# The first pair of products split a third time, with its operands fetched by DMA instead of by matmul

## The chip, the cores and the metric

The kernel runs on one core of one Trainium2 chip. The metric is the device time of one execution in microseconds (us). A core has five engines that run beside each other: TensorE (PE in the profile; its weight loads are PEld), VectorE (DVE), ScalarE (ACT), GpSimd (POOL) and SyncE (SP). DMAs are issued from the queues of SyncE, ScalarE and GpSimd. Matmuls write to PSUM banks; all other operands are in SBUF or in DRAM.

## The reference

```python
def reference(x, router_logits, expert_weights):
    probs = softmax(router_logits, axis=-1)          # [16, 512, 8]
    for e in range(8):
        expert_out = np.matmul(x, expert_weights[e]) # [16, 512, 512] @ [512, 2048]
        output += probs[:, :, e:e+1] * expert_out
    return output                                    # [16, 512, 2048], f32
```

With the 8192 tokens as rows this is one product of a matrix Z (8192 x 4096) by a matrix W (4096 x 2048). Z holds x times the routing weight of each of the eight experts side by side, W the experts' weights on top of each other. The inputs are f32; the kernel multiplies in f16 and accumulates in f32.

## The kernel before, in words

**Three levels of splitting.** The product is not computed block by block. Rows (256 tokens each, even and odd), the sum over experts (0 to 3, 4 to 7) and columns (two halves of 1024) are halved, and seven products of sums of blocks take the place of eight. They are called 1 to 7, and each runs for 16 pairs of row blocks (q from 0 to 15). `STEPS = (1, 5, 6, 2, 7, 3, 4)` is the same splitting a second time: inside a product there are seven steps of 8 matmuls, each with 128 x 128 of Z as the weight load and 512 columns of W. `by_thirds` is the third level: for a stage of two products, steps 1 and 5 of both (32 matmuls of 512 columns) are replaced by 14 small products of 4 matmuls with 256 columns. Their left operands are sums of the two products' z halves (`Thirds`, made on VectorE as tasks 5, 6, 3, 7), their right operands are sums of quarters of the weight block (`third_sums`).

**Stages.** `stages` lists the pairs of products in order of time, and `run(stage)` emits one. Stage 0 is product 1 of q = 2 and 3, stage 1 product 1 of q = 4 and 5, and so on up to stage 6. Before this change `thirds` holds stages 1 to 6 of these seven (line 1584), so stage 0 runs its 14 steps whole. Product 1 of q = 0 and 1 comes ahead of all stages and is computed directly: lines 266 to 358 make four blocks `z0` by matmul with diagonal matrices of routing weights (`early_z0`), and two loops over the column halves n with four experts e each run 16 matmuls per expert. The kernel starts there, since these need only a quarter of x's first rows, a tiny softmax and the first casts of weights.

**Operands of stage 0.** A z half is x transposed (`xT`) times the routing weights broadcast over partitions (`pT`); `times` makes one on VectorE. For stage 0, `early_xp1` (lines 286 to 294) makes both with TensorE: four 128-column matmuls against an identity for xT, one 512-column matmul of ones against diagonal tiles for pT, copied out of PSUM by VectorE and ScalarE. The routing weights for it come from a small softmax of its own (`early_p(1)`, on `lg0[1]`). For all later stages xT is made by DMA transposes on SyncE and pT is loaded, broadcast over the partitions, from `p_dram`. `softmax_of_all` (lines 309 to 322) fills `p_dram`: it runs the softmax of all logits on VectorE and ScalarE, casts it to f16 on ScalarE (lines 319 and 320), and stores it from SyncE in four DMAs.

**Weights.** `cast_block` and `cast_w` issue DMAs on GpSimd's queue that read f32 weights and write f16. The four blocks `b11` of product 1 and the eight early x blocks (`cast_x`) are issued in one row at the very start, lines 230 to 242. `behind` holds a DMA back until what was issued before it.

**What sets the order.** VectorE's and ScalarE's instructions keep program order throughout (`dve`, `act`); the other engines' do so from line 360 on. VectorE's work in the stages is a `queue` of tasks with assumed costs. `clock` holds the assumed time of TensorE and of VectorE; `slack` moves TensorE's clock on and emits tasks while VectorE's is behind, and `need` emits all tasks up to the one that TensorE is about to read. Lines 1599 to 1607 fill this queue for stage 0: z halves, the weight sums 6, 7 and 4 of product 1 (`inner_sums`), the differences `s2`.

Of the kernel before, what the change touches and what calls it, by code (L numbers as in the profile page):

```python
# [31 lines left out]
def kernel(  # L32
# [7 lines left out]
    nc = tc.nc  # L40
    P = 128
# [64 lines left out]
    def dve(i):  # L106
        last[i.ins.engine] = i.ins
        tc.keep_in_program_order(i)
# [3 lines left out]
    def tt(o, a, b, op):  # L112
        dve(nc.vector.tensor_tensor(out=o, in0=a, in1=b, op=op))  # L113
# [9 lines left out]
    def sp(o, i):  # L123
        note(nc.sync.dma_start(out=o, in_=i))
# [10 lines left out]
    def mm(ps, z, w, start, stop):  # L135
        note(nc.tensor.matmul(ps, z, w, start=start, stop=stop, skip_group_check=True))  # L136
# [80 lines left out]
    def cast_x(j):  # L217
        pool(xs0[:, ds(j, 2), :], x_f[ds(j * HQ, HQ), :].rearrange(ROWS[j // 4], p=P))

    def load_lg0(t):  # L220
        rows = lg_f.rearrange("(q h) e -> q h e", h=2 * HQ)[ds(2 * t, 2), 0:HQ]
        tile_ = lg0[t].rearrange("p (q j) e -> p q j e", j=2)
        if t == 0:
            sp(tile_, rows.rearrange("q (p j) e -> p q j e", p=P))
        else:
            for q in range(2):
                sp(tile_[:, q], rows[q].rearrange("(j p) e -> p j e", p=P))
    lg0 = [cpool.tile([P, 4, E], f32, name=f"lg0_{t}") for t in range(2)]
    load_lg0(0)
    cast_x(0)  # L230
    cast_x(2)
    ident = cpool.tile([P, P], f16, name="ident")
# [2 lines left out]
                            pattern=[[-1, P]], channel_multiplier=1)  # L235
    b11 = {kn: new_w() for kn in BLOCKS}
    with behind():
        for kn in BLOCKS[:3]:
            cast_block(11, kn, b11[kn], 2 if kn == (0, 0) else 1)
    cast_x(4)  # L240
    cast_x(6)
    cast_block(11, BLOCKS[3], b11[BLOCKS[3]])

    def early_p(t):
        if t == 0:
            return softmax(lg0[t], 4, cpool.tile([P, HE, 4], f16, name="ph0"))
        pf = softmax(lg0[t], 4, cpool.tile([P, HE, 4], f32, name="pf0"))
        odd = pf.rearrange("p e (q j) -> p e q j", j=2)[:, :, :, 1]
        tt(odd[:, 0:2], odd[:, 0:2], odd[:, 2:4], ADD)
        ph = cpool.tile([P, HE, 4], f16, name="ph1")  # L250
        dve(nc.vector.tensor_copy(ph, pf))
        return ph

    def diag(p):

        d = h_tile([P, 4, P], f16)
        tt(d, ident.unsqueeze(1).to_broadcast([P, 4, P]), p.to_broadcast([P, 4, P]), MUL)
        return d
# [5 lines left out]
            dve(nc.vector.tensor_copy(o, ps))  # L264

    z0 = [zpool.tile([P, HE, C, P], f16, name="z", tag="z") for j in range(4)]
    ph0 = [early_p(0)]

    def diag_e(e):
        return diag(ph0[0][:, e].unsqueeze(2))  # L270

    def early_z0(e, d):
        for j in range(4):
# [5 lines left out]
    ones = cpool.tile([P, P], f16, name="ones")  # L279
    nc.vector.memset(ones, 1.0)  # L280
    xp1 = [[xpool.tile([P, C, HQ], f16, name=name, tag="x") for name in ("xT", "pT")] for t in range(2)]

    def diag_j(j):
        return diag(ph0[1][:, :, ds(j % 4, 1)])

    def early_xp1(j, d):
        t, rows = j // 2 - 2, ds(j % 2 * P, P)
        ps = (bank, bank2)[j % 2]()
        for c in range(C):
            mm(ps[:, ds(c * P, P)], xs0[:, j, ds(c * P, P)], ident, c == 0, c == C - 1)  # L290
        evacuate(xp1[t][0][:, :, rows], ps.rearrange("p (c t) -> p c t", c=C), 0)
        ps = (bank, bank2)[j % 2]()
        mm(ps, ones, d.rearrange("p e t -> p (e t)"), True, True)
        evacuate(xp1[t][1][:, :, rows], ps.rearrange("p (e t) -> p e t", e=HE), 1)

    R = 4
    J = HQ // R
# [3 lines left out]

    def load_logits():
        dve(nc.vector.memset(lg_all[:, 0, 0:1], 0.0))
        dve(nc.vector.memset(lg0[1][:, 0, 0:1], 0.0))
        load_lg0(1)
        for r in range(R):
            sp(lg_all[ds(r * NHQ, NHQ)], lg_v[r])

    def softmax_of_all():

        pf = softmax(lg_all, J, h_tile([P, E, J], f32))
        pq = h_tile([P, HE, J], f32)
# [7 lines left out]
        act(nc.scalar.copy(ph[:, E:], pq))  # L320
        for r in range(R):
            sp(p_dram[:, :, ds(r * J, J)], ph[ds(r * NHQ, NHQ)])

    kept = [dram.tile([2, HQ, NB], f32, name=f"kept_{i}") for i in range(NI)]

# [5 lines left out]
    for n in range(2):  # L331
        ps = [bank2() if n == 0 and j < 2 else bank() for j in range(4)]
        for e in range(HE):
            if n == 0 and e < 2:
                early_z0(e + 2, ds_[e + 2])
                if e == 0:
                    ds_.append(diag_e(3))
            if n == 0 and e == 2:
                ph0.append(early_p(1))
                ds_ = [diag_j(j) for j in range(4, 8)]  # L340
                softmax_of_all()
                w, sums = inner_sums(b11, new_w())
                third = {1: third_sums(w[1])}
            for c in range(C):
                for j in range(4):
                    mm(ps[j], z0[j][:, e, c], b11[e // 2, n][:, e % 2 * C + c, :],
                       e + c == 0, e == HE - 1 and c == C - 1)
            if n == 1:
                for j in ((4, 5), (6, 7), (), ())[e]:
                    early_xp1(j, ds_[j - 4])  # L350
                if e == 0:
                    sums[5]()
                elif e == 1:
                    third[5] = third_sums(w[5])
        for j in range(4):
            o = half()
            act(nc.scalar.copy(o, ps[j]))
            sp(kept[j // 2][n].rearrange("(p j) m -> j p m", j=2)[j % 2], o)

    ordered[0] = True  # L360
    SLOT = 1.73
# [1 line left out]
    HP = HQ // 2  # L363
    LAG, LATE, LATE_TWOS = 0.3, 2.6, 1.6
    queue = deque()
    clock = {"pe": 0.0, "dve": 0.0}

    class Task:

# [429 lines left out]


    right = {r: Right() for r in (2, 5, 6, 7, 4, 3)}
    right[1] = Right(w, {p: Task(2.29, sums[p]) for p in (6, 7, 4)})
    lefts, xs, ps_, bases = {}, {}, {}, {}

    def xblock(h):
# [775 lines left out]
            post(p)  # L1581
    finish.step, finish.post = step_at_end, post_at_end

    for stage in range(1, ND):
        thirds[stage] = Thirds(*(p.left for p in stages[stage]), third)
    for stage in range(ND + 1, last2):
        thirds[stage] = Thirds(*(p.left for p in stages[stage]), third2)
# [9 lines left out]
    for stage in range(k3 + 1, end):  # L1597
        thirds[stage] = Thirds(*(p.left for p in stages[stage]), third3, room_w, False)
    need_first = [right[1].task[p] for p in (6, 7, 4)]
    for p in (2, 3):  # L1600
        lefts[1, p].queue_make(0)
    queue.append(need_first[0])
    for p in (2, 3):
        lefts[1, p].queue_s2()
    for p in (2, 3):
        lefts[1, p].queue_make(1)
    queue.extend(need_first[1:])
    start_loads(1)
    store_loads(0)
# [31 lines left out]
```

## Time and profile before

| what | us |
|---|---|
| median of three runs (lowest, highest) | 1351.76 (1351.49, 2032.81) |
| the profiled execution | 1351.78 |
| its span, first to last instruction | 1350.1 |
| TensorE busy | 1344.0 |
| VectorE busy | 1166.9 |
| ScalarE busy | 281.9 |
| GpSimd busy | 403.9 |

The span is what the profile shows; the profiled execution's own time is 1.7 us longer. One of the three runs took 2032.81 us and stands apart from the other two, which agree within 0.3 us. The lines of the profile use the program's names: `out<-in`, with the tile's name and without its number. `z` is an operand of Z, `w` a block of weights, `ps` and `pt` are PSUM banks, `d` the differences s2, `h` a scratch tile. Nearly every VectorE line stands under L113 and every matmul under L136, since two helpers record them; one tells them apart by tiles and shapes. The granted TensorE clock was 1.0 throughout.

### The profile page before, as it was taken

The page shows a single profiled execution, that of the slowest core. Times are in us where ns is not written, and L with a number is a line of the kernel's source. Part 1 is how long each engine was busy: PE and PEld are TensorE (multiplying, and loading weights), DVE is VectorE, ACT ScalarE, POOL GpSimd, SP SyncE. Part 2 cuts the span into 40 slices and gives each one's busy share as a digit, 9 for nine tenths or more (in the row PEclk, how much of TensorE's full clock was granted, in tenths as well). Part 3 has the DMA queues.
Part 4 walks back from the last instruction along what each step waited for, and adds up shares of the span by engine and source line. Part 5 has one row for each costly group of instructions (what it writes and reads, how often), then busy time and mean ns, then how long its engine had stood idle before and what let it go on. Part 6 is the DMA issues. An engine that isn't in the chain of part 4 may idle for free.

```text
span 1350.1 us, 19508 instructions
## 1 busy us (share of the span) xinstructions
PE 1344.0 (100%) x7122; PEld 694.3 (51%) x7122; DVE 1166.9 (86%) x1483; ACT 281.9 (21%) x593; POOL 403.9 (30%) x619
## 2 busy tenths in 40 slices
PE   9999999999999999999999999999999999999998
PEld 4465655565544444444444444554555455556564
DVE  7878898989989889797897889889898989898984
ACT  3342423223211111111111100110111111224331
POOL 3123322333323232323312112424334231232342
PEclk9999999999999999999999999999999999999999
DMA  9999989989899999999998889999999989999997
GB/s 181 242 222 240 239 264 242 291 284 290 247 329 282 323 288 286 295 306 265 318 325 265 295 313 189 243 239 216 244 249 226 219 219 310 308 178 230 262 163 132
DMA packets 185392, 346.26 MB, mean 256 GB/s; under 512 B 52176, under 2 KB 81616, under 8 KB 181200
## 3 DMA queue, kind: packets, MB, share of 16 engines
q0 software_dynamic: 84960, 176.72, 58.0%
q1 hardware_dynamic: 97024, 146.15, 35.4%
q10 hardware_dynamic: 3312, 22.15, 4.6%
q8 instruction: 55, 0.90, 0.3%
q14 instruction: 41, 0.34, 0.1%
HBM read 203.19 MB, written 174.26 MB: 280 GB/s over the span
## 4 chain that ended last, share of the span: by engine, by line
PE 98%; DMA 1%; POOL 0%; issue 0%; ACT 0%; POOLq 0%
PE ps L136 77%; PE pt L136 21%; DMA w<-in_expert_weights_dram 1%; POOL w L127 0%; ACT h L1578 0%; POOL ident L234 0%; POOLq L234 0%; POOLq L1625 0%
## 5 line engine op out<-in xcount | busy, mean ns | idle before, releaser
L136 PE MATMUL ps<-w,z 128*128 128x512 f16 (+1 forms) x3884 | 840.0, 372 | 0.0
L136 PEld LDWEIGHTS <-z 128*128 128x128 f16 x5236 | 512.3, 98 | 538.1 <-issue 1.1
L127 POOL DMA_DIRECT2D out_dram<-h x380 | 251.8, 679 | 723.9 <-ACT h L751 321.9
L113 DVE TENSOR_TENSOR h<-ps,h 128x512 f32<-128x512 f32 x318 | 214.9, 686 | 59.1 <-PE ps L136 58.0
L136 PE MATMUL pt<-w,z 128*128 128x512 f16 (+1 forms) x1304 | 253.2, 338 | 0.7 <-DMA w<-in_expert_weights_dram 0.7
L113 DVE TENSOR_TENSOR z<-xT,pT 128x2048 f16<-128x2048 f16 x188 | 226.8, 1217 | 2.2 <-DMA xT<-xs 2.2
L136 PE MATMUL ps<-w,d 128*128 128x512 f16 x880 | 200.7, 379 | 0.0
L738 ACT COPY h<-ps 128x512 f32<-128x512 f32 x102 | 59.8, 586 | 394.0 <-PE ps L136 394.0
L136 PEld LDWEIGHTS <-d 128*128 128x128 f16 x880 | 86.1, 98 | 96.3
L113 DVE TENSOR_TENSOR z<-z,d 128x2048 f16<-128x2048 f16 x110 | 131.8, 1217 | 0.0
L113 DVE TENSOR_TENSOR w<-w 128x1024 f16<-128x1024 f16 (+2 forms) x106 | 116.1, 1114 | 2.6 <-PE ps L136 1.0
L113 DVE TENSOR_TENSOR d<-z 128x1024 f16<-128x1024 f16 x110 | 74.1, 685 | 1.0
L113 DVE TENSOR_TENSOR h<-pt,h 128x512 f32<-128x512 f32 x75 | 51.3, 687 | 27.0 <-PE pt L136 23.9
L751 ACT COPY h<-ps 128x512 f32<-128x512 f32 x54 | 31.6, 586 | 203.5 <-PE ps L136 203.5
L113 DVE TENSOR_TENSOR ps<-ps,h 128x256 f32<-128x256 f32 (+1 forms) x84 | 50.6, 603 | 21.0 <-PE ps L136 15.1
L734 ACT COPY h<-ps 128x512 f32<-128x512 f32 x89 | 49.9, 599 | 70.1 <-PE ps L136 61.3
L127 POOL DMA_DIRECT2D kept<-h x56 | 30.6, 547 | 86.2 <-DVE h L113 48.7
L113 DVE TENSOR_TENSOR z<-z 128x2048 f16<-128x2048 f16 (+1 forms) x52 | 50.5, 978 | 1.5
L730 ACT COPY ps<-ps 128x512 f32<-128x512 f32 x47 | 26.8, 570 | 107.4 <-PE ps L136 59.5
L113 DVE TENSOR_TENSOR h<-h 128x512 f32<-128x512 f32 (+2 forms) x69 | 45.0, 675 | 0.1
L127 POOL DMA_DIRECT2D out_dram<-kept x40 | 42.0, 1150 | 0.2 <-issue 0.2
L136 PEld LDWEIGHTS <-h 128*128 128x128 f16 x384 | 37.6, 98 | 4.3
(109 smaller groups left out, 691.7 us busy)
## 6 DMA issues: line engine op xcount, KB each, us to landing
out_dram<-h POOLq DMA_DIRECT2D x380, 256.0 KB, 7.5
z<-z SPq DMA_DIRECT2D x56, 512.0 KB, 8.7
pT<-p_dram SPq DMA_DIRECT2D x93, 256.0 KB, 8.1
h<-kept SPq DMA_DIRECT2D x88, 256.0 KB, 7.2
w<-wd ACTq DMA_DIRECT2D x20, 1024.0 KB, 8.6
w<-in_expert_weights_dram POOLq DMA_DIRECT2D x33, 512.0 KB, 12.2
xT<-x SPq DMA_DIRECT2D x63, 256.0 KB, 7.8
h<-out_dram SPq DMA_DIRECT2D x60, 256.0 KB, 8.9
```

Source lines behind the costliest of these rows:

```text
L113: dve(nc.vector.tensor_tensor(out=o, in0=a, in1=b, op=op))
L127: note(nc.gpsimd.dma_start(out=o, in_=i, **how))
L136: note(nc.tensor.matmul(ps, z, w, start=start, stop=stop, skip_group_check=True))
L730: act(nc.scalar.copy(self.banks["b"], x))
L734: act(nc.scalar.copy(o[tn], q if p == 5 else x))
L738: act(nc.scalar.copy(o[TN[p]], b if p == 2 else x))
L751: act(nc.scalar.copy(o[tn], b))
```

## The change

Stage 0 joins the stages that are split a third time, and its operands come another way:

- The small softmax, the diagonal tiles, the 16 transposing and 4 broadcasting matmuls of `early_xp1` and their copies are gone, and so are the two loads of `lg0[1]`.
- `softmax_of_all` is emitted earlier, at the second expert of the first column half. Its four stores to `p_dram` are issued by ScalarE, behind the two casts.
- `second_x` issues four transposing DMAs on SyncE that make xT of stage 0 from the early x blocks 4 to 7. `second_p` issues two loads of pT of stage 0 from `p_dram` on ScalarE, behind the evacuations of the first column half.
- The casts of x blocks 4 to 7 go ahead of the second half of the third weight block.
- Weight sums 5 and 6 of product 1 are made in halves; the queue for stage 0 is now the first half of sum 6, then `thirds[0].queue()` (z halves 0, sums 5, 6, 3, 7, s2, z halves 1) with the second half of sum 6 put in behind the sums, then weight sums 7 and 4. VectorE's assumed clock starts at -7.5.

```diff
-    load_lg0(0)
+    lg0 = cpool.tile([P, 4, E], f32, name="lg0")
...
-        for kn in BLOCKS[:3]:
+        for kn in BLOCKS[:2]:
             cast_block(11, kn, b11[kn], 2 if kn == (0, 0) else 1)
+        cast_w(11, BLOCKS[2], 0, b11[BLOCKS[2]][:, ds(0, C), :])
     cast_x(4)
     cast_x(6)
+    cast_w(11, BLOCKS[2], 1, b11[BLOCKS[2]][:, ds(C, C), :])
     cast_block(11, BLOCKS[3], b11[BLOCKS[3]])
...
-        dve(nc.vector.memset(lg0[1][:, 0, 0:1], 0.0))
-        load_lg0(1)
...
         for r in range(R):
-            sp(p_dram[:, :, ds(r * J, J)], ph[ds(r * NHQ, NHQ)])
+            act(nc.scalar.dma_start(out=p_dram[:, :, ds(r * J, J)], in_=ph[ds(r * NHQ, NHQ)]))
+
+    def second_p():
+        for t, (_, p) in enumerate(xp1):
+            act(nc.scalar.dma_start(out=p, in_=p_dram[2 * t + 4, ds(P1, HE), :].partition_broadcast(P)))
+
+    def second_x():
+        for j in range(4):
+            note(nc.sync.dma_start_transpose(out=xp1[j // 2][0][:, :, ds(j % 2 * P, P)], in_=xs0[:, j + 4, :]))
...
                 if e == 0:
                     ds_.append(diag_e(3))
+                else:
+                    softmax_of_all()
+                    second_x()
             if n == 0 and e == 2:
-                ph0.append(early_p(1))
-                ds_ = [diag_j(j) for j in range(4, 8)]
-                softmax_of_all()
...
             if n == 1:
-                for j in ((4, 5), (6, 7), (), ())[e]:
-                    early_xp1(j, ds_[j - 4])
                 if e == 0:
-                    sums[5]()
+                    sums[5](ds(0, C))
+                    sums[5](ds(C, C))
...
+        if n == 0:
+            second_p()
...
-    clock = {"pe": 0.0, "dve": 0.0}
+    clock = {"pe": 0.0, "dve": -7.5}
...
-    right[1] = Right(w, {p: Task(2.29, sums[p]) for p in (6, 7, 4)})
+    right[1] = Right(w, {p: Task(2.29, sums[p]) for p in (7, 4)})
+    right[1].task[6] = Task(1.22, lambda: sums[6](ds(C, C)))
...
-    for stage in range(1, ND):
+    for stage in range(ND):
         thirds[stage] = Thirds(*(p.left for p in stages[stage]), third)
...
-    for p in (2, 3):
-        lefts[1, p].queue_make(0)
-    queue.append(need_first[0])
...
+    later(1.22, lambda: sums[6](ds(0, C)))
+    thirds[0].queue()
+    queue.insert(7, need_first[0])
     queue.extend(need_first[1:])
```

More of the change, by code (lines that the diff above doesn't have):

```diff
@@ L218, in cast_x @@
         pool(xs0[:, ds(j, 2), :], x_f[ds(j * HQ, HQ), :].rearrange(ROWS[j // 4], p=P))
[L220 to L228, printed above, removed]
-    load_lg0(0)
+    lg0 = cpool.tile([P, 4, E], f32, name="lg0")
+    sp(lg0.rearrange("p (q j) e -> p q j e", j=2),
+       lg_f.rearrange("(q h) e -> q h e", h=2 * HQ)[ds(0, 2), 0:HQ].rearrange("q (p j) e -> p q j e", p=P))
     cast_x(0)
@@ L237 @@
     with behind():
-        for kn in BLOCKS[:3]:
+        for kn in BLOCKS[:2]:
             cast_block(11, kn, b11[kn], 2 if kn == (0, 0) else 1)
+        cast_w(11, BLOCKS[2], 0, b11[BLOCKS[2]][:, ds(0, C), :])
     cast_x(4)
     cast_x(6)
+    cast_w(11, BLOCKS[2], 1, b11[BLOCKS[2]][:, ds(C, C), :])
     cast_block(11, BLOCKS[3], b11[BLOCKS[3]])
[L244 to L252, printed above, removed]
     def diag(p):
@@ L266 @@
     z0 = [zpool.tile([P, HE, C, P], f16, name="z", tag="z") for j in range(4)]
-    ph0 = [early_p(0)]
+    ph0 = softmax(lg0, 4, cpool.tile([P, HE, 4], f16, name="ph0"))
     def diag_e(e):
-        return diag(ph0[0][:, e].unsqueeze(2))
+        return diag(ph0[:, e].unsqueeze(2))
     def early_z0(e, d):
@@ L277, in early_z0 @@
             evacuate(z0[j][:, e], ps.rearrange("p (c t) -> p c t", c=C), j)
-    ones = cpool.tile([P, P], f16, name="ones")
-    nc.vector.memset(ones, 1.0)
     xp1 = [[xpool.tile([P, C, HQ], f16, name=name, tag="x") for name in ("xT", "pT")] for t in range(2)]
[L283 to L294, printed above, removed]
     R = 4
@@ L1599 @@
     need_first = [right[1].task[p] for p in (6, 7, 4)]
-    for p in (2, 3):
-        lefts[1, p].queue_make(0)
-    queue.append(need_first[0])
[L1603 to L1606, printed above, removed]
+    later(1.22, lambda: sums[6](ds(0, C)))
+    thirds[0].queue()
+    queue.insert(7, need_first[0])
     queue.extend(need_first[1:])
```

## The prediction

> **What bounds the kernel now.** First the page: which engine never rests, and what the chain that ended last is made of.
>
> ```profile
> span 1350.1 us, 19508 instructions
> PE 1344.0 (100%) x7122; PEld 694.3 (51%) x7122; DVE 1166.9 (86%) x1483; ACT 281.9 (21%) x593; POOL 403.9 (30%) x619
> PE 98%; DMA 1%; POOL 0%; issue 0%; ACT 0%; POOLq 0%
> ```
>
> TensorE is busy throughout and the chain is TensorE for 98%. So TensorE time taken out is won in full, and a TensorE wait put in is lost in full; other engines count only where TensorE waits for them. All that the change touches lies in the first 65 us, so I went on to the timeline of TensorE there, then to the busy time of stretches cut where TensorE changes its work (columns: stretch, length, then busy time of PE, PEld, DVE, ACT, POOL).
>
> ```profile
> 17.33 0.59 PE L136 MATMUL ps<-w,z 128*128 128x512 f16 x2
> 18.26 0.59 PE L136 MATMUL pt<-w,z 128*128 128x512 f16 x2 [0.33 <-DMA w<-in_expert_weights_dram]
> ...
> 33.83 10.52 PE L136 MATMUL ps<-w,z 128*128 128x512 f16 x48
> 44.19 3.62 PE L136 MATMUL pt<-w,z 128*128 128x512 f16 x16
> 47.64 3.62 PE L136 MATMUL ps<-w,d 128*128 128x512 f16 x16
> 51.09 7.07 PE L136 MATMUL ps<-w,z 128*128 128x512 f16 x32
> ```
> ```profile
> 28.62:29.49 0.87, 0.87 (x11) 0.64 (x10) 0.45 (x1) 0.23 (x1) 0.00 (x0) 1.00 1.25 207
> 32.95:33.83 0.88, 0.88 (x12) 0.64 (x11) 0.46 (x1) 0.24 (x1) 0.00 (x0) 1.00 1.38 214
> ```
>
> From 44.19 to 47.64 there are 16 matmuls, 0.216 us each. The row of 48 holds the last 32 matmuls of the direct blocks and 16 of stage 0, so stage 0 starts at 33.83 + 32 x 0.216 = 40.74. Its step 2 starts at 51.09, and step 7 of its first product 16 matmuls later, at 54.54. I measure the change against that 54.54.
>
> **What TensorE is spared.** The two short stretches are the transposes and broadcasts by matmul that the change drops: 0.87 + 0.88 = 1.75 us. Steps 1 and 5 of both products are 32 matmuls, 6.91 us. What replaces them is seen in stage 1, which is already split a third time:
>
> ```profile
> 64.91 1.04 PE L136 MATMUL pt<-w,z 128*128 128x256 f16 x8
> ...
> 71.02 3.62 PE L136 MATMUL ps<-w,d 128*128 128x512 f16 x16
> ```
>
> That is 6.11 us, so 0.80 is spared. The wait at 18.26 is for a weight cast:
>
> ```profile
> 5.13 13.09 DMA w<-in_expert_weights_dram
> ```
>
> The dropped second small logits tile took 512 rows of 32 B (8 experts in f32) out of the same DMA engines just ahead of it. The gain is between 0 and 0.5 us (the pair at 17.33 is two matmuls of 0.216, so the next could have started at 17.76); I take 0.3. Sum: 2.85 us. If nothing new waited, stage 0 would start at 40.74 - 1.75 - 0.3 = 38.7, and the profiled time would be 1348.9.
>
> **What is late next: the routing weights.** They now make a round trip. Before, pT of stage 0 came out of a matmul; now it needs softmax of all logits, two casts, four stores to DRAM and a load.
>
> ```profile
> 13.84 1.29 DVE L264 CAST z<-ps 128x512 f16<-128x512 f32 x2 [2.35 <-PE ps L136]
> ...
> 19.28 0.68 DVE L200 TENSOR_REDUCE h<-h 128x64 f32<-128x512 f32 x1
> ```
> ```profile
> 25.25 0.40 ACT L320 CAST h<-h 128x256 f16<-128x256 f32 x1
> ```
> ```profile
> 9.44 1.43 SPq L124 DMA_DIRECT2D h<-in_router_logits_dram  x3
> 25.68 2.67 SPq L124 DMA_DIRECT2D p_dram<-h  x4
> 28.46 14.22 SPq L124 DMA_DIRECT2D kept<-h  x8
> 42.73 1.24 SPq L124 DMA_DIRECT2D pT<-p_dram  x2
> 45.03 6.28 SPq L432 DMA_TRANSPOSE xT<-xs  x4
> ```
>
> VectorE keeps program order, and the softmax now follows the last early z casts, which end at 13.84 + 1.29 = 15.13. The small softmax and four diagonal tiles between 15.1 and 19.28 are gone. Its input is there in time: the last of the four large logits loads, issued at 10.42, landed 5.9 us later at 16.3 (row below), with the 32 B rows ahead of it; without them I take it as in by 15.1 (1.2 later if not). From the first reduction to the first store were 25.68 - 19.28 = 6.4 us. So the stores are issued, now by ScalarE, from 21.5 to 24.2.
>
> The landing is the weak point. The answers on DMA, for 10.4 to 10.9 (loads of logits), 27.7 to 28 (the last store), 25.6 to 29.7, and 29.8 to 33:
>
> ```profile
> h<-in_router_logits_dram SPq DMA_DIRECT2D x1, 64.0 KB, 5.9
> p_dram<-h SPq DMA_DIRECT2D x1, 48.0 KB, 8.9
> q1 hardware_dynamic: 1, 0.00, 0.0%
> ...
> q0 software_dynamic: 621, 0.61, 112.1%
> q1 hardware_dynamic: 610, 0.08, 30.2%
> ```
>
> Until 29.7 not one packet of the stores had moved (4.1 us after the first issue); then they went one for one with the weight casts, 610 in 3.2 us, 190 per us. Four stores of 48 KB in 128 B pieces are 1536 packets: 8.1 us. In the changed kernel the casts run the whole time: 21.5 + 4.1 + 8.1 + 0.5 to land = 34.2. The transposes are then a third flow, so up to 35.5. By the last store's own 8.9 us it would be 23.5 + 8.9 = 32.4. I take 34.5. ScalarE waits for it before issuing the loads; behind them on ScalarE are the four evacuations after the second column half, needed at 38.7, so that wait itself costs nothing. The loads, at 42.7 and at 51.4, and over the whole run:
>
> ```profile
> pT<-p_dram SPq DMA_DIRECT2D x2, 256.0 KB, 5.3
> pT<-p_dram SPq DMA_DIRECT2D x2, 256.0 KB, 4.2
> DMA to landing us min/median/max: 3.3/8.1/20.0
> ```
>
> With 4.7, the first pT lands at **L = 39.2**, the second 0.6 later. Bounds: 32.4 + 3.3 = 35.7, and 35.5 + 5.9 = 41.4.
>
> The Trainium skill, "DMA: Bandwidth & Descriptors", section "Latency and other measured facts", speaks for a fast trip: about 0.6 us to the first byte of a hardware-queued transfer and some 2 us of fixed cost. By an estimate from that page the whole trip would be in by about 30 and the first rival below would come true; the 4.1 us without a packet says otherwise, under this load.
>
> The other additions. First the x casts that the transposes read, as GpSimd issues them, and the answers on their landing:
>
> ```profile
> 8.06 0.79 POOL L127 DMA_DIRECT2D w<-in_x_dram  x1
> 10.21 0.72 POOL L127 DMA_DIRECT2D w<-in_x_dram  x1 [1.36 <-DMA w<-in_expert_weights_dram]
> ```
> ```profile
> w<-in_x_dram POOLq DMA_DIRECT2D x1, 256.0 KB, 18.7
> w<-in_x_dram POOLq DMA_DIRECT2D x1, 256.0 KB, 17.9
> ```
>
> They landed at 26.8 and 28.1, 1.3 us apart for 256 KB, so a 512 KB cast takes 2.6. **Transposes:** the x casts now stand one 512 KB cast earlier in that row, and land at about 24.2 and 25.5. Four transposes at 1.57 us of issue (6.28 for 4) are out by 31, and with up to 7 us to land (an estimate: a third more than the 5.3 of pT) are all in by 38, ahead of L; two us more would still be hidden behind the first half's 1.2 us. The kept stores, next on SyncE, go out 2 us later; nobody waits for them. **Weights:** the second half of the third block lands in the place of the second x cast, at about 28, and is needed at 28.62 - 0.3 = 28.3, because no matmul of the dropped kind stands before it any more; sharing with the transposes may cost it 1 us, and that wait only takes from the one below. **Fourteen small products** bring ScalarE eight short copies more for the four casts of pT that go, hidden since TensorE waits for VectorE there, and VectorE the work below.
>
> **What TensorE then waits for.** With pT at L, VectorE has to do in this order: two z halves, the sums 5, 6, 3, 7, half of weight sum 6, two s2, four small evacuations, two z halves, weight sums 7 and 4, then the operand of step 7. From the VectorE timeline:
>
> ```profile
> 42.78 2.36 DVE L113 TENSOR_TENSOR z<-xT,pT 128x2048 f16<-128x2048 f16 x2
> 45.05 4.49 DVE L113 TENSOR_TENSOR w<-w 128x4096 f16<-128x4096 f16 x2
> 49.45 2.36 DVE L113 TENSOR_TENSOR z<-z,d 128x2048 f16<-128x2048 f16 x2
> ...
> 68.67 0.87 DVE L113 TENSOR_TENSOR ps<-pt,z 128x256 f32<-128x256 f32 x2 [2.52 <-PE pt L136]
> ...
> 74.65 0.69 DVE L113 TENSOR_TENSOR h<-z 128x1024 f16<-128x1024 f16 x1
> ...
> 77.31 1.29 DVE L113 TENSOR_TENSOR d<-z 128x1024 f16<-128x1024 f16 x2
> ```
>
> Two z halves 2.3; four sums 77.31 - 74.65 = 2.66; half a weight sum 1.1; two s2 1.2; four evacuations 1.6; two z 2.3; two weight sums 4.4; the operand 1.2. Sum 16.8, with semaphores 17.0. TensorE's own way to that step is a start at L + 1.2, 8 us for the split with its waits for the sums, and four steps of 1.73: L + 16.1, so VectorE decides: step 7 starts at **L + 17.0**. Before, VectorE was done with these sums at 51.8, 2.7 us ahead of step 7, because the matmuls of 28.6 and 33 gave it pT. So the change costs (L + 17.0) - 54.54 = L - 37.5. With L = 39.2 that is **+1.7 us**: the 2.85 spared are lost in about 4.5 us of waits in stage 0. Later VectorE has slack again: sums of stage 1 end at about L + 26, before that stage starts at L + 27.5. The profiled execution took 1351.78 (span 1350.1 and 1.7 around it), the median is 1351.76; so 1351.8 + 1.7 = **1353.5**.
>
> **Rivals.**
> *The trip is short* and TensorE keeps what it is spared. Even from L = 37.5, all 2.85 us won from L = 34.6 on: 1349 to 1351.8, at L = 35.7 1350.0. For it: the last store took 8.9 us, not 11; ScalarE's queue is empty, while SyncE's had loads ahead. Against: the 4.1 us with no packet. Chance 0.25.
> *The DMA engines are shared by three.* Casts, transposes and stores each get a third until the casts end at about 36, and the transposes and 1 MB of kept stores go on beside the loads: L of 41 to 43, so +3.5 to +5.5, 1355.3 to 1357.3. It decides from L = 41. The Trainium skill, same page, section "Issuing engines are not separate DMA queues", has that queues of several engines end on the same 16 DMA engines, so that moving the stores to ScalarE's queue brings no bandwidth; the one-for-one packet rows agree. Chance 0.2.
> *It does not do what it says*: large logits in only at 16.3, or the transposes later than pT, so that the earlier softmax is not earlier. Worth at most 1.2 us, 1354.7; inside the forecast's range.
>
> **How the numbers follow.** Forecast (L from 37.5 to 41, 1351.8 to 1355.3): 0.52. Short trip 0.25; three flows 0.2; 0.03 for something else. With both signs likely the range reaches into both: **1349.6 to 1356.4**; the likeliest case alone is 1351.8 to 1355.3. Two per cent is 27 us, about what a measurement of this kernel can tell from no change, and several times any wait here: faster 0.01, same 0.98, slower 0.01.
>
> **What would show it.** Gone: the 128-wide matmuls at 28.6 and 33. Stage 0 with 56 matmuls of 256 columns. VectorE idle for some 6 us before the first z<-xT,pT, ended by the DMA of pT at about 39; ScalarE idle until the stores land near 34.5; TensorE with about 2 us of wait at the start of stage 0, more between its small products, and one before step 7 that VectorE ends. I am wrong if pT lands before 36, if the first z waits for the transposes, or if the time is lost outside stage 0.

## The result

The changed kernel takes 1358.42 us (median of six, 1356.74 to 1359.94), the kernel before, run beside it, 1351.63. The ratio is 1.0051, interval 1.0037 to 1.0065: half a per cent slower, within the 2% that I called the same, but outside the range on record (1349.6 to 1356.4) at the slow end. The profiled execution of the changed kernel took 1356.74, span 1355.0: 4.96 more than the profiled 1351.78 before. So two amounts are to be explained: 5.0 in the profile, and some 1.7 more in the typical execution.

The head of the page, for the lines quoted of before:

```profile
span 1355.0 us, 19510 instructions
PE 1343.0 (99%) x7126; PEld 695.0 (51%) x7126; DVE 1164.4 (86%) x1476; ACT 282.1 (21%) x596; POOL 403.8 (30%) x619
PE 95%; DVE 0%; ACT 0%; issue 0%
```

TensorE is busy 1.0 us less and the span is 4.9 us longer: it waits. Where, the timeline of TensorE from 36 to 60 shows (start, length, work, and in brackets the idle time ahead of it and what ended it):

```profile
42.94 1.38 PE L136 MATMUL pt<-w,z 128*128 128x256 f16 x8 [4.55 <-DVE z L113]
44.99 1.04 PE L136 MATMUL ps<-w,h 128*128 128x256 f16 x4 [0.68 <-DVE h L113]
45.82 1.58 PE L136 MATMUL pt<-w,h 128*128 128x256 f16 x8
47.24 0.60 PE L136 MATMUL ps<-w,h 128*128 128x256 f16 x4
...
49.86 0.60 PE L136 MATMUL pt<-w,z 128*128 128x256 f16 x4 [0.28 <-DVE ps L113]
...
51.60 3.62 PE L136 MATMUL ps<-w,d 128*128 128x512 f16 x16
55.06 3.62 PE L136 MATMUL ps<-w,z 128*128 128x512 f16 x16
59.66 2.55 PE L136 MATMUL ps<-w,z 128*128 128x512 f16 x11 [0.98 <-DVE z L113]
```

Measured from the regular distance between matmuls (0.108 us at 256 columns, 0.216 at 512), the four waits are 4.71, 0.99, 0.44 and 1.15: 7.29. The direct blocks end at 42.94 - 4.71 = 38.23, 2.51 earlier than before. Most of the first 20 small products are twice as far apart as later ones: 45.82 to 47.24 is 1.42 for 8, where 8 are 0.87. Over the first 20 of them that is 1.15. So step 7 moves by -2.51 - 0.80 + 7.29 + 1.15 = +5.13. It starts at 59.66 instead of 54.54, +5.12, and nothing in this profile waits behind it.

What ended the waits is VectorE, and what VectorE itself waited for stands in its timeline:

```profile
14.78 0.69 DVE L200 TENSOR_REDUCE h<-h 128x64 f32<-128x512 f32 x1
...
41.65 2.55 DVE L113 TENSOR_TENSOR z<-xT,pT 128x2048 f16<-128x2048 f16 x2 [9.80 <-DMA pT<-p_dram]
44.24 0.69 DVE L113 TENSOR_TENSOR h<-z 128x1024 f16<-128x1024 f16 x1
...
51.37 0.43 DVE L113 TENSOR_TENSOR ps<-ps,z 128x256 f32<-128x256 f32 x1 [0.90 <-PE ps L136]
51.71 2.35 DVE L113 TENSOR_TENSOR z<-xT,pT 128x2048 f16<-128x2048 f16 x2
53.98 4.49 DVE L113 TENSOR_TENSOR w<-w 128x4096 f16<-128x4096 f16 x2
58.38 2.35 DVE L113 TENSOR_TENSOR z<-z,d 128x2048 f16<-128x2048 f16 x2
```

The softmax starts at 14.78, 4.5 us earlier than before, and still VectorE stands idle for 9.8 us until pT lands. The time in between is in the queue of ScalarE and the landings (queue, operation, KB, us from issue to landing):

```profile
21.19 2.67 ACTq L290 DMA_DIRECT2D p_dram<-h  x4
...
37.98 0.84 ACTq L294 DMA_DIRECT2D pT<-p_dram  x2
```
```profile
p_dram<-h ACTq DMA_DIRECT2D x1, 48.0 KB, 14.2
pT<-p_dram ACTq DMA_DIRECT2D x1, 256.0 KB, 3.5
```

The last store was issued at 23.22 and landed 14.2 us later, at 37.45. Then pT was issued at 37.98 and landed at 41.53. The DMA queues from 27 to 35 show why a store took so long (packets, MB, share; q0 carries GpSimd's casts, q1 SyncE's transposes, q10 ScalarE's stores):

```profile
q0 software_dynamic: 1171, 1.15, 84.8%
q1 hardware_dynamic: 1138, 0.28, 26.7%
q10 hardware_dynamic: 1171, 0.14, 12.7%
```

Three flows move packet for packet, 146 per us each, whatever a packet holds: the stores' 128 B count like the casts' 1 KB. The Trainium skill, "DMA: Bandwidth & Descriptors", section "Queues, rings and completion order", says that each DMA engine goes round the queue rows at packet granularity; these three rows agree with it.

### The profile page after: what moved, and what is told of

It reads as the page before. It is cut to its first block, busy times and chain, and to the rows that moved or that the text cites. A ratio compares the mean times of both kernels' runs of the same rounds, so it can differ in the third digit from the quotient of the medians.

```text
span 1355.0 us, 19510 instructions
## 1 busy us (share of the span) xinstructions
PE 1343.0 (99%) x7126; PEld 695.0 (51%) x7126; DVE 1164.4 (86%) x1476; ACT 282.1 (21%) x596; POOL 403.8 (30%) x619
## 4 chain that ended last, share of the span: by engine, by line
PE 95%; DVE 0%; ACT 0%; issue 0%
PE ps L136 75%; PE pt L136 20%; DVE z L113 0%; ACT h L1556 0%
## 5 line engine op out<-in xcount | busy, mean ns | idle before, releaser
L136 PE MATMUL pt<-w,z 128*128 128x512 f16 (+1 forms) x1288 | 248.5, 336 | 4.9 <-DVE z L113 4.5
L136 PEld LDWEIGHTS <-h 128*128 128x128 f16 x416 | 40.9, 99 | 6.6 <-DVE h L113 1.4
L127 POOL DMA_DIRECT2D out_dram<-kept x40 | 42.1, 1144 | 0.3 <-issue 0.2
```

The source lines that it names most:

```text
L127: note(nc.gpsimd.dma_start(out=o, in_=i, **how))
```

## The experiments

All of them compute the reference's function; none leaves a part of it out. L is the landing of the first pT, "first z" VectorE's first z half of stage 0. Medians stand beside those of the kernel before on the same chip. The experiments ran on three chips, on which the kernel before took 1351.34 to 1351.47, so they can be compared with each other.

### The changed kernel again

> The changed kernel once more, beside the kernel before, on the same chip as the experiments. Every theory expects 5 to 8 us over the kernel before. If the late routing weights are the cause, the landing of the second pT and the start of step 7 of the first product in stage 0 move together from run to run, step 7 about 18 us after the first pT.

1359.25 against 1351.34, 1.0064 (1.0040 to 1.0088). The profiled execution took 1359.81, 3.07 more than the first profile. L is 42.31 and step 7 starts at 60.51, 0.85 later. The other 2.23 are far behind stage 0. The chain of waits there is short; first TensorE's timeline, then ScalarE's:

```profile
146.00 0.60 PE L136 MATMUL pt<-w,z 128*128 128x256 f16 x4
148.67 0.60 PE L136 MATMUL pt<-w,z 128*128 128x256 f16 x4 [2.07 <-ACT ps L959]
```
```profile
147.76 0.58 ACT L704 COPY h<-ps 128x512 f32<-128x512 f32 x1 [4.24 <-DMA kept<-h]
148.24 0.38 ACT L959 COPY ps<-pt 128x256 f32<-128x256 f32 x1
```

ScalarE needs a scratch tile h, and that tile is free only when the store of an earlier result from it has landed. This store was issued at 131.26 and landed at 147.68, 16.4 us later. In the first profile of the same kernel the store at that place took 13.9 and TensorE did not wait. So this is a second loss, in stage 4, that some executions have: 0.85 + 2.23 = 3.08 accounts for this one. That the 1.7 us between the first profile and the median are of this kind, and of a pT that lands later in some executions, is likely and not shown. Similar losses stand in the profiles of other late kernels below (1.85 at 146.7, 0.8 to 1.0 at 425 to 427, 1.40 at 667). Of the eight profiles of kernels with a late pT five have a wait of 0.8 or more behind stage 0; of the six others, that of before among them, none has one above 0.25. That they come from stage 0's lateness is likely, but how is not shown.

### xT by matmul again, no transposes

```diff
-    def second_x():
-        for j in range(4):
-            note(nc.sync.dma_start_transpose(out=xp1[j // 2][0][:, :, ds(j % 2 * P, P)], in_=xs0[:, j + 4, :]))
+    def second_x(j):
+        ps = (bank, bank2)[j % 2]()
+        for c in range(C):
+            mm(ps[:, ds(c * P, P)], xs0[:, j, ds(c * P, P)], ident, c == 0, c == C - 1)
+        evacuate(xp1[j // 2 - 2][0][:, :, ds(j % 2 * P, P)], ps.rearrange("p (c t) -> p c t", c=C), 0)
...
             if n == 1:
+                for j in ((4, 5), (6, 7), (), ())[e]:
+                    second_x(j)
```

> As the changed kernel, but xT of stage 0 comes from matmuls again (0.87 us of TensorE), so no transposing DMA runs beside the stores of the routing weights. Theory (the routing weights are late because weight casts, transposes and their own stores share the DMA engines): the last store lands near 34.3 and not at 37.5, pT near 38.5, so 1.5 to 3 us over the kernel before. Rival (the stores are slowed by the casts alone, transposes do not matter): pT stays near 41.5, 5 to 7 us over. Rival (the third split in itself costs, by VectorE's new order): 5 to 7 us over.

1356.97 against 1351.34, 1.0040 (1.0025 to 1.0055). My theory expected the stores to land early without the transposes; the last one landed at 38.12. From 29 to 33 the queues show what took the transposes' place:

```profile
q0 software_dynamic: 377, 0.38, 55.3%
q1 hardware_dynamic: 373, 0.70, 52.1%
q10 hardware_dynamic: 376, 0.05, 8.4%
```

q1 now carries the kept stores, 2 KB a packet (0.70 MB in 373), and all three flows get 94 packets per us. SyncE, free of transposes, issues the kept stores from 25.4 on, not from 31.9. So it is not transposes as such: both third flows took a third of the packets, and the one with larger packets left the small ones even fewer. L is 41.44 and step 7 starts at 59.55: nothing is won.

### Stores and transposes on one queue

```diff
-            act(nc.scalar.dma_start(out=p_dram[:, :, ds(r * J, J)], in_=ph[ds(r * NHQ, NHQ)]))
+            sp(p_dram[:, :, ds(r * J, J)], ph[ds(r * NHQ, NHQ)])
...
-                    second_x()
+                    with behind():
+                        second_x()
```

> As the changed kernel, but the four large stores are issued by SyncE and the transposes behind them on the same queue, so that stores and transposes no longer run beside each other: the stores share the DMA engines with the weight casts alone. Sharing by three is the cause of the late stores: their packets go at 190 per us instead of 140 and are through by 34, the last store lands near 34.5 instead of 37.5. If the load of pT stands only behind its stores, it goes out near 34.6 and the first z starts near 39: 2.5 to 4.5 us over the kernel before. If it stands behind a transpose as well (eight places before it), the transposes now come after the stores, it goes out near 39 and the time is 5 to 8 us over.

1356.56 against 1351.42, 1.0046 (1.0028 to 1.0065). From 27 to 33 there are two flows, and the stores have half of the packets:

```profile
q0 software_dynamic: 1163, 1.15, 112.6%
q1 hardware_dynamic: 1163, 0.14, 30.7%
```

That is 194 per us, the rate that my sum had taken. The last store landed at 35.63, 1.8 us earlier, although the first was issued 0.7 later (21.90 against 21.19), and pT was issued at 35.65. It then needed 4.8 us, beside the last transposes (in by 37.64) and four kept stores: L = 40.45, 1.1 earlier, and step 7 at 58.83. The sharing by three is thus worth 2.5 us at the stores, counted from their first issue, and about 1 at L. The time is 5.1 over and not the 2.5 to 4.5 of the theory: the last store landed 1.1 later than the 34.5 expected, pT took longer, and the profiled execution (1358.80) has waits of 0.30, 1.02, 1.40 and 0.30 far behind stage 0.

### Small stores first

```diff
+        act(nc.scalar.copy(ph[:, 0:E], pf))
+        for r in range(R):
+            act(nc.scalar.dma_start(out=p_first[:, :, ds(r * J, J)], in_=ph[ds(r * NHQ + 4, 3), 0:HE]))
...
-            act(nc.scalar.dma_start(out=p, in_=p_dram[2 * t + 4, ds(P1, HE), :].partition_broadcast(P)))
+            act(nc.scalar.dma_start(out=p, in_=p_first[2 * t].partition_broadcast(P)))
+        for r in range(R):
+            act(nc.scalar.dma_start(out=p_dram[:, :, ds(r * J, J)], in_=ph_all[0][ds(r * NHQ, NHQ)]))
```

A DRAM tile `p_first` takes only the three row blocks that stage 0's pT may read, 48 packets instead of 1536, and the large stores go behind the loads. The transposes stay.

> As the changed kernel, but the routing weights of row blocks 4 to 6 are stored first, in four small stores to a DRAM tile of their own, the loads of pT wait for these alone, and the four large stores go behind the loads. Theory (late routing weights): the small stores land near 26, pT near 32, and then xT decides, whose last transpose lands near 38; first z near 35.5, second near 38, so 0 to 2 us over the kernel before. Rival (transposes are late in the same way and decide anyway): no better than 4 us over. Rival (the third split in itself costs): 5 to 7 us over.

1358.06 against 1351.34, 1.0050 (1.0035 to 1.0065): nothing gained. The last of the 48 packets started at 29.5, and yet ScalarE issued pT at 38.26:

```profile
21.95 3.63 ACTq L291 DMA_DIRECT2D p_first<-h  x4
...
38.26 0.84 ACTq L297 DMA_DIRECT2D pT<-p_first  x2
```

The built program says for what it waits. DMAs of SyncE and ScalarE share eight completion semaphores, DMAHW0 to DMAHW7, in turn; a DMA that takes one over waits until its last user has landed. In the changed kernel:

```
SP  L124 DMACopy kept_0_140<-h_363 128x512 [waits DMAHW5_49,Activation_49]
SP  L124 DMACopy kept_0_140<-h_366 128x512 [waits DMAHW6_49,Activation_49]
ACT L294 DMACopy pT_135<-p_dram_138 128x1024 [waits DMAHW4_49,DMAHW3_49,DMAHW7_49,DMAHW2_49,DMAHW1_49]
```

In the turn, the five loads of logits have DMAHW0 to 4, the transposes 5, 6, 7 and 0, and the stores 1 to 4. So four of the waits of pT are the four stores, and DMAHW7 is the third transpose, whose data pT does not touch. The trace agrees in both kernels: in the changed one the transposes landed at 31.60, 35.38, 37.89 and 38.31, and the first kept store was issued at 31.92, the second at 35.44, pT at 37.98, the third kept store at 38.37. Here they landed at 32.54, 37.44, 38.16 and 38.63, followed by 32.62, 37.51, 38.26 and 38.70. So in the changed kernel the stores (37.45) and the third transpose (37.89) each hold pT back to about 38, and taking away one of them alone leaves the other.

### Both: small stores first, and xT by matmul

The edits of this section's second and fourth experiments together.

> As the changed kernel, with the four small stores of row blocks 4 to 6 ahead and xT by matmul. In the run with small stores and transposes the load of pT was issued 0.1 us after the landing of the third transpose, though the small stores' packets had passed 8 us earlier. Theory A (a transfer issued from SyncE or ScalarE waits until the one eight places before it among those two queues has landed, so the load stood behind a transpose that it has nothing to do with): without transposes the load goes out near 30 and pT lands near 34.5; TensorE then waits 0 to 1 us in stage 0, and the time is 0.5 to 2.5 us under the kernel before. Theory B (the load waits for its data only, and small stores to DRAM are slow to land under the weight casts): the load still goes out near 38, 4 to 6 us over the kernel before.

1352.86 against 1351.37, 1.0011 (1.0002 to 1.0020). pT is issued at 29.66:

```profile
29.66 0.86 ACTq L297 DMA_DIRECT2D pT<-p_first  x2
```

and lands at 35.93, 5.6 us earlier than in the changed kernel. Step 7 comes 3.93 earlier, and the profiled execution takes 1352.75, 3.99 less, although xT by matmul gives TensorE 0.87 us of work back. (The medians differ by 5.6 as well, but in them are the losses behind stage 0; that the two numbers agree is chance.) Each edit alone had left L at 41.4 or later. So the late routing weights are most of the loss, and the third transpose held them back as the stores did. VectorE does not take pT up at once:

```profile
32.84 0.39 PE L136 MATMUL pt<-ident,w 128*128 128x128 f16 x4
```
```profile
34.25 3.75 DVE L113 TENSOR_TENSOR w<-w 128x1024 f16<-128x1024 f16 x5
37.92 2.35 DVE L113 TENSOR_TENSOR z<-xT,pT 128x2048 f16<-128x2048 f16 x2
```

The first z starts 2 us after pT, behind sums of weight quarters that themselves stood behind the late transposes by matmul; step 7 starts at 55.73, behind a wait of 1.15.

### The third split alone

The kernel before with stage 0 split a third time (`thirds` from 0, the changed kernel's queue), operands by matmul as before.

> The third split alone: the kernel before with stage 0 split a third time and VectorE's queue in the changed order, operands by matmul as before, softmax and stores as before. Theory (late routing weights, the split is sound): first z at about 35.5 to 37, step 7 at about 53.5 to 54.5, 0.8 us of TensorE spared, so 0 to 1 us under the kernel before. Rival (the split costs by itself): 2 us or more over.

1353.40 against 1351.34, 1.0015 (1.0006 to 1.0025). No DMA is new here, pT is there, and it still costs 2.1 (0.8 in the profiled execution, whose direct blocks end at 39.76, 0.98 earlier than those of before):

```profile
41.69 1.03 PE L136 MATMUL pt<-w,h 128*128 128x256 f16 x8 [0.46 <-ACT ps L966]
...
45.13 0.60 PE L136 MATMUL pt<-w,z 128*128 128x256 f16 x4 [0.22 <-DVE ps L113]
...
54.92 7.30 PE L136 MATMUL ps<-w,z 128*128 128x512 f16 x33 [0.98 <-DVE z L113]
```

The first z comes only at 37.27, and the waits of 0.63, 0.39 and 1.14 are more than the 0.80 that the split spares. The split adds work to VectorE ahead of step 7, and VectorE is what step 7 waits for.

### The changed kernel without the third split

```diff
-    for stage in range(ND):
+    for stage in range(1, ND):
...
+    for p in (2, 3):
+        lefts[1, p].queue_make(0)
+    queue.append(need_first[0])
...
```

> As the changed kernel, but stage 0 keeps its 14 whole steps (no third split there), VectorE's queue in the old order. If the late pT alone is the loss: stage 0 starts when the first z half is done, at about 42.9, and TensorE runs at half clock for some 3 us: step 7 at about 58, so 3 to 4.5 us over the kernel before, less than the changed kernel, because no sums of a third split stand between pT and the later steps on VectorE. If the third split is worth its 0.8 us even here: not less than the changed kernel's 5 to 7.

1357.63 against 1351.37, 1.0042 (1.0027 to 1.0057). pT lands at 42.28, stage 0 starts at 43.69, and no wait is left ahead of step 7, which starts at 59.0. That is 4.5 us later than before; with a wait of 1.85 at 146.67 it makes the 6.3 of this median, more than the 3 to 4.5 expected. With pT this late, the split decides little either way.

### Weight sum 4 behind step 7's operand

```diff
+    at(0, 0, lambda: (queue.remove(need_first[2]), queue.append(need_first[2])))
```

> As the changed kernel, but weight sum 4 of product 1 (2.2 us, first read in the last step) goes behind the operand of step 7 in VectorE's order. My chain has VectorE decide when step 7 starts: then the wait of 1.1 us before step 7 goes, 0.8 to 1.2 us less than the changed kernel on the same chip. Rival (TensorE's own way decides): no difference beyond 0.3 us.

1356.84 against 1351.37, 1.0042 (1.0027 to 1.0056). The wait of 1.15 before step 7 is gone:

```profile
52.69 3.62 PE L136 MATMUL ps<-w,d 128*128 128x512 f16 x16
56.14 8.15 PE L136 MATMUL ps<-w,z 128*128 128x512 f16 x37
```

The profiled execution, 1356.70, is no faster than the first one of the changed kernel, but in it pT landed at 42.59, 1.06 later: the two cancel. The changed kernel was not run on this chip, so the time alone decides nothing. Step 7 now starts when TensorE gets there, at 59.59; its operand was ready at about 58.5 (the first of two z<-z,d that start at 57.26). TensorE took 15.6 us from its first small product to step 7, where the regular distances add up to 13.0 and a wait to 0.5. The other 2.1 went to a granted clock of 0.50, which stood from 42.1 to 48.7 in this profile.

### A clock kept warm

```diff
+    idle = bank()
+    for i in range(20):
+        mm(idle, ident, b11[1, 1][:, i % K8, :], True, True)
```

Twenty extra matmuls, read by nobody, fill TensorE's long wait.

> As the changed kernel, with 20 matmuls of 512 columns whose result nobody reads put between the last direct block and stage 0, where TensorE waits 4.7 us. They take 4.3 us, so TensorE is not idle for more than 0.5 us and keeps its clock. If the half clock after the wait costs time: the small products run at 0.108 us from the start, and the time is 0.5 to 1.5 us under the changed kernel's. If VectorE's chain hides it: within 0.3 us of the changed kernel.

1358.45 against 1351.37, 1.0049 (1.0034 to 1.0064): the same time as without them. The question was the doubled distance of the first small products. By stretches of the changed kernel (stretch, length, busy time of PE, PEld, DVE, ACT, POOL, then granted clock):

```profile
41.00:43.60 2.60, 0.66 (x6) 0.61 (x7) 1.85 (x2) 0.00 (x0) 0.00 (x0) 0.98 1.06 407
43.70:46.90 3.20, 2.52 (x13) 1.38 (x12) 2.96 (x5) 1.02 (x3) 0.00 (x0) 0.50 1.02 321
47.00:50.00 3.00, 2.72 (x26) 2.28 (x25) 3.00 (x6) 1.03 (x3) 0.00 (x0) 1.00 1.40 286
```

After 4.7 us without a matmul the granted clock was 0.50 for some 3 us; it fell when the first six small products had already gone at the full rate. In the second profile of the same kernel it stood at 0.50 from 42.1 to 48.7, twice as long. The Trainium skill, "TensorE: Matmul & The Clock Gate", section "What's actually happening", puts the halving behind an idle window of about 3.4 us; the rows agree. With the extra matmuls the clock stayed at 1.00:

```profile
43.70:46.90 3.20, 1.66 (x12) 1.01 (x12) 2.82 (x4) 0.80 (x3) 0.00 (x0) 1.00 1.05 369
```

TensorE then did 12 matmuls in 1.66 us, where 13 had taken 2.52, and waited longer between them (0.78, 1.31, 0.35, 1.01 and 1.14). Step 7 follows L by 18.3 us here, by 18.1 in the first profile of the changed kernel and by 18.2 in the second with its longer half clock. So the half clock is real and costs nothing in this order: VectorE's chain covers it. Where TensorE decides step 7, as in the two experiments before this one, it does cost.

### The best orders

Three kernels try the edits in a better order. In the first, the third split alone (operands by matmul) has weight sum 5 begun one expert earlier and weight sum 4 behind step 7's operand. Against the kernel before, beside the edits of the third split alone:

```diff
+            if n == 0 and e == 3:
+                sums[5](ds(0, C))
...
             if n == 1:
+                if e == 0:
+                    sums[5](ds(C, C))
                 for j in ((4, 5), (6, 7), (), ())[e]:
                     early_xp1(j, ds_[j - 4])
                 if e == 0:
-                    sums[5]()
+                    pass
...
+    at(0, 0, lambda: (queue.remove(need_first[2]), queue.append(need_first[2])))
```

> The third split with operands by matmul, and VectorE's order made for it: the two halves of weight sum 5 go ahead of the copies of xT (where VectorE idled 0.9 us for TensorE), and weight sum 4 behind the operand of step 7. If VectorE's chain is the only thing that took the split's gain: first z at about 35.5 instead of 37.3, no wait before step 7, the split's 0.8 us are won: 0 to 1 us under the kernel before. If the split costs something later in the kernel as well (a wait for scratch tiles in later stages): still 0.5 to 2 us over.

1351.98 against 1351.42, 1.0002 (0.9994 to 1.0011). No wait is left at step 7, and 0.63, 0.39 and 0.23 elsewhere: the split's 0.80 is spent on its own waits. The first z comes at 37.75 and not at the 35.5 expected: VectorE now waits 1.79 us for the second two transposes by matmul.

The second is small stores and xT by matmul, with the same order.

> Small stores first, xT by matmul, third split, and the same order on VectorE (halves of weight sum 5 early, weight sum 4 behind step 7's operand). First pT near 36, first z near 36, TensorE through stage 0 without waits beyond 0.3 us; it is spared 0.8 us by the split and 0.87 us by the dropped broadcasts: 1 to 2.5 us under the kernel before. If something later takes it back: within 1 us of the kernel before.

1351.27 against 1351.42, 0.9998 (0.9990 to 1.0007). Waits of 0.20, 0.42 and 0.96 are left in stage 0, and the first z, at 37.33 and not near 36, is still 1.4 behind pT. Of the 1 to 2.5 us expected nothing is clear.

The third also moves all four transposes by matmul to the first expert:

```diff
-                for j in ((4, 5), (6, 7), (), ())[e]:
+                for j in ((4, 5, 6, 7), (), (), ())[e]:
```

> Edit: as e14 (small stores first, xT by matmul, weight sum 5 begun a block of experts earlier, weight sum 4 behind the operand of step 7), with all four transposes by matmul in the first expert of the second column half instead of two in the first and two in the second. In e14 pT landed at 35.91 and VectorE came to the first z only at 37.33: it had idled 2.61 us until 32.46 for the second two transposes and did 3.75 us of quarter sums behind them. Theory A (stage 0 starts when VectorE has pT and nothing else left ahead of it): the quarter sums end at about 35.1, the first z starts at pT's landing, 35.9 to 36.0, and 1.2 to 1.6 us of the waits of stage 0 (0.20, 0.42 and 0.96 in e14) go: 1349.7 to 1350.4, that is 1.0 to 1.7 us under the kernel before. Rival (pT lands later when VectorE's or TensorE's work is moved ahead, or the waits between the small products are set by the products' own chain and not by the start): the same time as e14, 1350.9 to 1351.7.

1350.72 against 1351.47, 0.9991 (0.9981 to 1.0001). The quarter sums are done before pT lands, and of TensorE's waits after 36 only one above 0.15 us is left, 0.63:

```profile
31.17 3.75 DVE L113 TENSOR_TENSOR w<-w 128x1024 f16<-128x1024 f16 x5
35.63 1.22 DVE L113 TENSOR_TENSOR z<-xT,pT 128x2048 f16<-128x2048 f16 x1 [0.72 <-DMA pT<-p_first]
```

The profiled execution took 1350.25 (span 1348.5), 1.5 less than that of before. Of this the edits account for 0.87 + 0.80 - 0.63 = 1.04. The medians differ by 0.75, and 1350.72 lies between what theory A and its rival expected. The interval just reaches 1: it may be faster than the kernel before, by less than a tenth of a per cent, which is not shown, and it is clearly faster than the changed one.

## Why the prediction was wrong

The mechanism was the forecast one: TensorE is spared work, pT comes late, VectorE stands idle for it and its chain decides when step 7 starts. The steps that failed are sizes in that sum, above all the landing of the stores, and a loss behind stage 0 for which the sum had no term.

**What TensorE is spared** came out near the sum, 2.51 + 0.80 = 3.31 against 2.85, but in part by luck. The dropped matmuls (1.75) and the split (0.80) are as summed. The direct blocks also start 0.48 earlier (9.49 instead of 9.97), and the wait of 0.5 at 18.26, of which I had taken 0.3, is gone. Neither is shown to come from the change: the third split alone, which keeps the second logits tile, starts them at 9.48 and has no such wait, while the changed kernel with weight sum 4 moved, which has dropped that tile, still waits 0.32 at 18.17. Nothing waited for the third weight block: its second half was in at 26.84 (I had 28), since the x casts ahead of it landed at 22.92 and 24.19 (24.2 and 25.5).

**The start of the trip** was right: softmax at 14.78 (I had 15.1), first store at 21.19 (21.5), first packet at 25.1, 3.9 us after the issue (4.1).

**The landing of the stores is the step that failed.** I took 190 packets per us, a rate at which two flows share, and 34.5 for the last landing, with 35.5 as the end for three flows. There were three flows nearly all the way, at 146 per us, and the landing was 37.45: 1.95 beyond my outer bound. The 1536 packets took from 25.13 to 35.77, 10.6 us and not 8.1. The landing came 1.7 after the last of them and not 0.5, the value of the kernel before; it is 1.3 to 2.1 in the six profiles with large stores and transposes beside them, and 0.45 to 0.55 in the four without. The experiment with one queue gives back the two flows, their 194 per us, and a landing of 35.63. My rival "the DMA engines are shared by three" is what happened at the stores. Its numbers, L of 41 to 43 and 1355.3 to 1357.3, hold the measured 41.53 and the profiled 1356.74, though not the median, and partly by luck: it had slow loads where a semaphore and fast loads came. I had seen the one-for-one rows, and the transposes that I put into SyncE's queue myself from 23 on, and still gave the rival 0.2.

**"All in by 38, ahead of L; two us more would still be hidden"** was right about the time of the transposes (38.31) and wrong about its price. No data of theirs is needed by then, but pT's issue stands behind the third one's completion semaphore. That wait is not in the diff and not in my sum. The experiment with small stores shows it alone: 38.26 with the stores long through.

**pT itself** was faster than I took, 3.55 against 4.7. The casts of x were in by 37.69, just before it was issued; with small stores and xT by matmul, among the casts, it took 6.3. Stores +2.95, from their landing to pT's issue +0.53 and the load -1.15 make L = 41.53 instead of 39.2, +2.3.

**The chain after L** was sized 17.0 and measured 18.1. Its operations cost what I had summed. What I left out is the last small evacuation, which waits 0.90 for TensorE's last small product, and the second pT, 0.25 behind the first z. That VectorE and not TensorE decides step 7 was right: in the six profiles with a late pT and this order step 7 follows L by 18.1 to 18.4, and moving sum 4 removes the wait there.

**The sum**: 2.3 for L and 1.1 for the chain are 3.4 on top of +1.7, 5.1 in all; step 7 moved by 5.12 and the profiled time by 4.96.

**"Later VectorE has slack again"** and my warning of time lost outside stage 0: this profile loses nothing there, but the second one loses 2.23 in stage 4, for a scratch tile. I compared one profile with a median, which held for the kernel before within 0.02 us. In the changed kernel the first profile was the fastest of six, and the median lies 1.7 higher. Even the first profile lies 0.3 above the range; the median lies 2.0 above it, and 1.7 of that is the part that the forecast had no term for. Its cause beyond the slow store of a kept result in stage 4 stays open.

**The other rivals.** The short trip did not happen, nor did it in any version that was run with the large stores ahead of pT. With 48 packets instead of 1536 and no transposes it does (pT issued at 29.66). The rival's price is not borne out by that alone: for L = 35.7 it had 1350.0, and with pT at 35.93 in VectorE's old order the profiled time is 1352.75. The best version, with pT at 35.6 and 1350.25, is another kernel, with xT by matmul and a new order. What the rival and my sum both left out is that the third split in this order costs more in waits than its 0.80, even with pT in time. "It does not do what it says" was wrong: the softmax is earlier by all that was intended.

## What to carry to other kernels

A DMA round trip put in place of a matmul is priced by the packets of all flows that will be in the engines at that time, the ones that the change itself adds included, and in these traces each flow counted by packets, not by bytes. Before moving a DMA, list what else shares its completion semaphores: with eight in turn, as here, a load can wait for a transfer that it has nothing to do with. And when an operand becomes late, sum the work of the engine that makes it, with the engine's own waits for the consumer, down to the first step that it delays.

## What was not expected of the hardware and the program

- Three flows shared the engines one to one to one at 146 packets per us each with pieces of 128 B, 256 B and 1 KB (0.14, 0.28 and 1.15 MB in the same 8 us), and at 94 each when one had 2 KB pieces.
- No more than eight DMAs of SyncE and ScalarE together, and eight of GpSimd, are outstanding in this program. GpSimd's eleventh cast was issued at 9.71, 0.28 after the third had landed (9.43), and the twelfth to the fifteenth each 0.28 to 0.29 after the fourth to the seventh.
- A store's landing came 1.7 us after its last packet: the last of the 1536 packets started at 35.77, and the last landing is at 37.45. Without transposes beside the stores it was 0.5: 36.05 and 36.59 in the kernel before, 37.57 and 38.12 with xT by matmul.
- The first packet of the stores moved 3.9 to 4.2 us after the first issue in every one of these traces, behind the casts: 25.13 after 21.19 in the changed kernel, 25.91 after 21.90 on one queue, 26.12 after 21.90 with small stores and xT by matmul.
- 4.7 us without a matmul cost about 3 us at half clock in one profile and nearly 7 in another of the same kernel, and hiding it gained nothing.
